# One packed array for the streamed weight tiles, a new start order, and eight unread products

## The chip, the cores and the metric

The kernel runs on one core of a Trainium2 chip. The metric is the device time of one execution in microseconds (us); lower is better. Beside the median of several timed runs there is one profiled execution, from which all rows in this document come.

## The reference

Three blocks run one after the other on x, 256 tokens of width 1024. Only the first steps of the first block matter here; the rest is named.

```python
def ssd_shortconv_layer_mixer(x, w_in, conv_w, conv_b, dt_bias, a_log, d_skip, norm_w, sc_conv_w, w_out):
    proj = x @ w_in
...
    z, xbc, dt_raw = proj[..., :o1], proj[..., o1:o2], proj[..., o2:o3]
    sc_b, sc_c, sc_h = proj[..., o3:o4], proj[..., o4:o5], proj[..., o5:]
    y_ssd = ssd_mixer(z, xbc, dt_raw, conv_w, conv_b, dt_bias, a_log, d_skip, norm_w)
    y_sc = sc_b * causal_dwconv(sc_c * sc_h, sc_conv_w)
    return jnp.concatenate([y_ssd.astype(x.dtype), y_sc.astype(x.dtype)], axis=-1) @ w_out
```

After it come a layer norm, a gated feed-forward layer and a gate (block one, first layer), the same with sliding-window attention (second layer), then a block with two mixers and 32 experts of which each token takes four, then a block with two kinds of attention. `dt_raw` is a product with 16 columns: one per head.

## The kernel before

Everything is float32. x is held transposed, as 128 partitions by 8 groups of features by 256 tokens (`xf`). A product with a weight matrix is made of three products of rounded halves: ScalarE rounds a tile to `wh` (line 295), VectorE or GpSimd subtracts to get `wl` (line 296), x is split in the same way into `xh` and `xl` (`resplit`, lines 707 to 712, by `split`), and TensorE multiplies `xh` by `wh`, `xl` by `wh` and `xh` by `wl` (line 493, reached by `dense_F` and its like).

The weights outside the experts are streamed by the class `Stream`. `weight_plan` lists the tiles in the order in which they are used, as (name, first row, row groups, first column, columns, split or not), and `pieces` cuts them into at most 2048 values per partition, that is, 1 MB. The first tile of the plan has 16 columns and 8 row groups (64 KB): it makes `dt_raw`, in 24 narrow products. Then come two tiles of 512 KB and full tiles. `Stream.load` fills a ring of eight buffers: while there is room, it takes the next tile of the plan and issues its transfer on SyncE's queue. Room is made when the last split of a tile has been issued. The expert tiles are streamed by another class, `Experts`, from arrays that are already contiguous per partition.

The program's order is the order in which the Python code calls the engines; no scheduler reorders it. A transfer whose completion is counted on one of eight semaphores is issued only when the earlier transfer on that semaphore has landed. `run` (from line 2450) issues at the start two transfers of x, of 512 KB each, then `st.load()`; ScalarE issues four small transfers from `consts` (cols, rows, exp_b, positions). `consts` also builds the identity `ident` on VectorE (line 405). Then `ssd_layer` splits x in four quarters and begins with the narrow tile (`dense_F` with n=16, line 752).

In the transfer of a tile, each partition gets one run of n values per row group, n being the tile's columns: 2 KB for 512 columns, 64 bytes for the narrow tile.

Of the kernel before, what the change touches and what calls it, by code (L numbers as in the profile page):

```python
# [22 lines left out]
F32 = mybir.dt.float32  # L23
# [10 lines left out]
T = 256  # L34
# [30 lines left out]
def _cols(v):  # L65
    v = np.asarray(v)
    return np.ascontiguousarray(v.reshape(-1, v.shape[-1] // 128, 128).transpose(2, 0, 1).reshape(128, -1))


def _freq():  # L70

    f = np.ones((128, 2), np.float32)
    for i, half in enumerate((32, 16)):
        inv = (10000.0 ** (-np.arange(half) / half)).astype(np.float32)
        f[:, i] = np.tile(inv, 128 // half)
    return f


def pack(I):
    I = {k: np.asarray(v) for k, v in I.items()}  # L80
    A = {}
    A["xT"] = np.ascontiguousarray(I["x"][0].T)
    A["pT"] = np.ascontiguousarray(I["p"][:, 0].transpose(0, 2, 1))
    hq = np.concatenate([np.arange(h * 64, h * 64 + 64) for h in HPERM])
    A["w_in_mix"] = I["w_in_mix"][0]
    A["w_out_mix"] = I["w_out_mix"][0]
    A["w_qkv"] = np.concatenate([I["w_qkv"][0][:, hq], I["w_qkv"][0][:, 1024:]], axis=1)
    A["w_o"] = np.ascontiguousarray(I["w_o"][0][hq])
    for i in range(2):
        for n in ("w_ffn_gate", "w_ffn_up", "w_ffn_down", "w_ple", "w_ple_gate"):  # L90
            A[f"{n}{i}"] = I[n][i]
    A["ada_p"] = I["ada_w_2"][0][:, :2048]
    A["ada_t"] = np.concatenate([I["ada_w_2"][0][:, 2048:], I["w_ada_3"][0]], axis=1).T
    A["c_rows"] = np.concatenate([I["c_2"], I["c_3"]], axis=1)
    A["w_in_2"] = I["w_in_2"][0]
    A["lora"] = np.concatenate([np.concatenate([I["decay_up_2"][0], I["iclr_up_2"][0]], axis=0), I["gate_up_2"][0]], axis=1)
    A["w_out_2"] = np.concatenate([I["w_out_2"][0][512:], I["w_out_2"][0][:512]])
    A["router_w"] = I["router_w_2"][0]

    A["exp_w1"] = I["exp_w1_2"][0].reshape(32, 4, 2, 128, 2048).transpose(0, 1, 3, 2, 4).reshape(-1, 4096)  # L100
    A["exp_w2"] = I["exp_w2_2"][0].reshape(32, 2, 4, 128, 1024).transpose(0, 1, 3, 2, 4).reshape(-1, 4096)
    A["exp_b1"] = np.ascontiguousarray(I["exp_b1_2"][0].reshape(32, 4, 512).transpose(1, 0, 2)).reshape(128, 512)
    A["exp_b2"] = I["exp_b2_2"][0]
    A["positions"] = I["positions_3"]
    A["w_in_3"] = I["w_in_3"][0]
    A["w_uq"] = I["w_uq_3"][0]
    A["w_ukv"] = I["w_ukv_3"][0]
    A["w_o_mla"] = I["w_o_mla_3"][0]
    A["w_o_moba"] = I["w_o_moba_3"][0]
    A["w_out_3"] = I["w_out_3"][0]  # L110
    bq = I["b_qkv"][0]
    c = {
        "conv_w": _cols(I["ssd_conv_w"][0]), "conv_b": _cols(I["ssd_conv_b"]), "sc_w": _cols(I["sc_conv_w"][0]),
        "ssd_nw": _cols(I["ssd_norm_w"]), "lnm_g": _cols(I["ln_mix_g"]), "lnm_b": _cols(I["ln_mix_b"]),
        "lnf_g": _cols(I["ln_ffn_g"]), "lnf_b": _cols(I["ln_ffn_b"]), "b_ple": _cols(I["b_ple_gate"]),
        "b_qk": _cols(np.concatenate([bq[hq], bq[1024:1280]])), "b_o": _cols(I["b_o"]),
        "d_skip": _cols(np.repeat(I["ssd_d"], 64, axis=1)),
        "norm1_g": _cols(I["norm1_g_2"]), "norm2_g": _cols(I["norm2_g_2"]), "ada_b": _cols(I["ada_b_2"]),
        "mu": _cols(I["shift_mu_2"]), "w0": _cols(I["decay_w0_2"]), "a0": _cols(I["iclr_a0_2"]),
        "k_k": _cols(I["k_k_2"]), "k_a": _cols(I["k_a_2"]), "r_k": _cols(I["r_k_2"].reshape(1, -1)),  # L120
        "lnx_w": _cols(I["lnx_w_2"]), "lnx_b": _cols(I["lnx_b_2"]),
        "q_g": _cols(np.concatenate([I["q_norm_g_2"]] * 2, axis=1)), "k_g": _cols(np.concatenate([I["k_norm_g_2"]] * 2, axis=1)),
        "sb_g": _cols(I["sb_out_g_2"]), "b_ada": _cols(I["b_ada_3"]), "c2": _cols(I["c_2"]), "c3": _cols(I["c_3"]),
        "g_pre": _cols(I["g_pre_3"]), "g_post": _cols(I["g_post_3"]), "g_ql": _cols(I["g_q_lat_3"]),
        "g_kv": _cols(I["g_kv_lat_3"]), "b_merge": _cols(I["b_merge_3"]), "freq": _freq(),
    }
    A["cols"] = np.concatenate([c[k] for k, _ in _COLS], axis=1)
    r = {
        "dt_bias": I["ssd_dt_bias"], "a_log": I["ssd_a_log"],
        "sinks": I["attn_sinks"][:, HPERM], "b_v": I["b_qkv"][:, 1280:],  # L130
        "router_b": I["router_b_2"],
    }
    A["rows"] = np.concatenate([r[k].reshape(1, -1) for k, _ in _ROWS], axis=1)
    return {k: np.ascontiguousarray(v) for k, v in A.items()}


# [91 lines left out]
    return [c for e in P for c in ([e] if e == "end" else pieces(*e))]  # L228


def pieces(name, r0, nk, c0, n, split):

    h = min(nk, 2048 // n)
    return [(name, r0 + k * 128, min(h, nk - k), c0, n, split) for k in range(0, nk, h)]


class Stream:


    def __init__(self, kb, plan, ring=8):  # L240
        self.kb, self.ring = kb, ring
        self.plan = []
        self.units = []
        self.fence = []
        unit = 1024
        for e in plan:
            if e == "end":
                self.fence.append(len(self.units))
                continue
            i = len(self.plan)  # L250
            self.plan.append(e)
            name, r0, nk, c0, n, split = e
            h = nk if not split else max(1, unit // n)
            for k in range(0, nk, h):
                self.units.append((i, k, min(h, nk - k), k + h >= nk, split))
        self.raws = {}
        self.splits = {}
        self.nsplit = self.used = 0
        self.pending = None
        self.rest = kb.nc.vector  # L260
        self.room, self.nload = ring, 0
# [7 lines left out]
            self._retire(self.pending)  # L269
            self.pending = None  # L270

    def load(self):

        kb = self.kb
        while self.room and self.nload < len(self.plan):
            i = self.nload
            self.nload += 1
            self.room -= 1
            name, r0, nk, c0, n, split = self.plan[i]
            t = kb.wpool.tile([128, nk, n], F32, name=f"w_{name}_{i}", tag="w")  # L280
            src = kb.A[name][r0:r0 + nk * 128, c0:c0 + n].rearrange("(k p) n -> p k n", p=128)
            kb.nc.sync.dma_start(t, src)
            self.raws[i] = t

    def _split(self, u):
# [83 lines left out]
class KB:  # L369
    def __init__(self, tc, A, out, stages, dbg=None):  # L370
        self.tc, self.nc, self.A, self.out, self.stages = tc, tc.nc, A, out, stages
        self._dbg = dbg
        self.bg = None
        self.late = (None, None, ())
        self.queue, self.done = [], set()
# [339 lines left out]
    def ssd_layer(self, xf):  # L715
        nc, pp = self.nc, self.pp
        es = ExitStack()
        P = es.enter_context(self.pool("ssd", 1))
        X = self.xpool
        x = self.resplit(xf, X)  # L720

        def padded(n):
# [109 lines left out]
    def state_space(self, P, xs, bc, v):  # L832

        nc, pp, X = self.nc, self.pp, self.xpool
        dt, da, ea, dte = (v[n] for n in ("dt", "da", "ea", "dte"))
# [16 lines left out]
        xdt = self.tl(P, [128, 2, 1024], F32, "xdt")  # L852
        xe = self.tl(X, [128, 2, 1024], F32, "xn")
        xde = xe[:, 0]
# [72 lines left out]
        while not self.x_done:  # L927
            yield
        self.yx = yx = (self.tl(X, [128, 8, T], F32R, "xh"), self.tl(X, [128, 8, T], F32R, "xl"))
        sq = self.tl(X, [128, 8, T], F32, "xn")  # L930
        for k in range(0, 8, 2):
# [83 lines left out]
    def attention(self, P, heads, bias, scale):  # L1015
# [7 lines left out]
        for i in range(n + 3):  # L1023
            if i < n:
# [5 lines left out]
                for b in range(2):  # L1030
                    nc.vector.tensor_reduce(m[:, b:b + 1], p[:, B[b]], axis=AX.X, op=OP.max)  # L1031
                nm = self.tl(P, [128, 2], F32, "an", bufs=2)
# [1417 lines left out]
    def run(self):  # L2450
        nc, tc = self.nc, self.tc
        with ExitStack() as es:
# [17 lines left out]
            self.tl = tl  # L2470
            self.st = Stream(self, weight_plan([n for n in self.stages if n != "third"]))
            xf = self.tl(self.fpool, [128, 8, T], F32, "xf")
            for k in (0, 4):
                nc.sync.dma_start(xf[:, k:k + 4], self.A["xT"][k * 128:k * 128 + 512].rearrange("(k p) n -> p k n", p=128))
            self.st.load()
            nc.scalar.preload_act_table_set("natural_log_exp_and_others")
            self.consts()
# [6 lines left out]
            if "ssd" in self.stages:  # L2484
                xf, x, ready = self.ssd_layer(xf)
                xf, x = self.ffn_ple(0, xf, x, ready)
                self.dbg("xc0", xf)
            else:
                stat = None
                x = self.resplit(xf, self.xpool)  # L2490
            if "att" in self.stages:
                xf, x, ready = self.att_layer(xf, x)
                xf, stat = self.ffn_ple(1, xf, x, ready)
# [7 lines left out]
            if "mix" in self.stages:  # L2501
                xf, stat = self.mixer(xf, stat)
                self.dbg("xd", xf)
            es.close()
            if "moe" in self.stages:
                xf, stat = self.moe(xf, stat)
# [16 lines left out]
ALL = ("ssd", "att", "mod", "mix", "moe", "third")  # L2523
# [14 lines left out]
```

## Time and profile before

| what | before |
|---|---|
| median of 3 runs | 2304.8 us (2302.57 to 2306.72) |
| the profiled execution's own time | 2310.93 us |
| its span, first to last instruction | 2308.8 us |
| TensorE busy | 2149.8 us, 93% |
| VectorE, ScalarE, GpSimd busy | 45%, 31%, 20% |
| mean granted TensorE clock | 0.969 |
| read from memory | 614.9 MB |

The profiled execution is one run of the program, a little slower than the median of the timed runs. Its span leaves out what lies before the first and after the last instruction, 2.1 us here. The busy shares are means over stages with different limits: a share of 93% doesn't say what any one stretch waits for. Expert tiles make up two thirds of the bytes, and they are read in the span's second half.

### The profile page before, as it was taken

To read this page: it belongs to the slowest core of one execution; us is meant where nothing else is said; L and a number is where in the kernel's file an instruction comes from. 1 tells how busy PE (TensorE), PEld (TensorE's weight loads), DVE (VectorE), ACT (ScalarE), POOL (GpSimd) and SP (SyncE) were. 2 spreads that over 40 slices of the span, in tenths; PEclk is the share of its full clock that TensorE was granted. 3 is DMA by queue.
4 is the path that set the end of the run, shared out by engine and by line. 5 is a ranking of instruction groups with operands and counts; after the bars stand their busy time and mean duration, and the time that the engine had idled before them with its cause. 6 is when DMAs were issued, how large, how long until landed. Compare 5 with 4: busy or idle time off the path is not lost.

```text
span 2308.8 us, 31649 instructions
## 1 busy us (share of the span) xinstructions
PE 2149.8 (93%) x13226; PEld 1513.6 (66%) x13226; DVE 1034.6 (45%) x1937; ACT 725.8 (31%) x1169; POOL 454.1 (20%) x220
## 2 busy tenths in 40 slices
PE   7999999989999987888899999999999999989996
PEld 7897898887898887778444444344433333367886
DVE  6674676555677658755222222322222211133653
ACT  5434544445544553333111111111111111033542
POOL 2322232233232234221000000000000000046454
PEclk9999999999999989989999999999999999999998
DMA  8434777532777632204799999999999999964320
GB/s 294 158 128 142 265 252 282 186 128 68 264 257 285 242 122 89 74 1 173 320 427 427 427 423 427 428 427 427 427 428 427 427 428 427 427 225 143 113 71 19
DMA packets 122339, 618.05 MB, mean 268 GB/s; under 512 B 8624, under 2 KB 17712, under 8 KB 97616
## 3 DMA queue, kind: packets, MB, share of 16 engines
q1 hardware_dynamic: 119008, 612.33, 67.6%
q10 hardware_dynamic: 3184, 3.65, 0.5%
q8 instruction: 106, 1.74, 0.3%
q14 instruction: 41, 0.34, 0.0%
HBM read 614.90 MB, written 1.05 MB: 267 GB/s over the span
## 4 chain that ended last, share of the span: by engine, by line
PE 34%; DMA 12%; DVE 3%; issue 1%; ACT 1%; POOL 0%; ACTq 0%; DVEq 0%; POOLq 0%; SPq 0%
PE acc L493 21%; DMA expert<-exp_w 12%; PE py L493 10%; PE tp L493 2%; DVE an L1034 1%; PE tp L2015 0%; POOL wl L296 0%; DVE pr L1065 0%; ACT pr L1057 0%; DVE am L1031 0%; PE tp L2007 0%; DVE qf L2443 0%; DVE ot L2377 0%; DVE r4h L505 0%; DVE kz L2350 0%
## 5 line engine op out<-in xcount | busy, mean ns | idle before, releaser
L493 PE MATMUL acc<-xh,wh 128*128 128x256 f32 (+1 forms) x1736 | 498.8, 291 | 16.1 <-ACT wh L295 13.3
L493 PE MATMUL acc<-xh,wl 128*128 128x256 f32 (+2 forms) x1704 | 488.5, 287 | 21.1 <-POOL wl L296 11.7
L493 PE MATMUL acc<-xl,wh 128*128 128x256 f32 (+1 forms) x1736 | 491.9, 287 | 0.6 <-DVE xl L1263 0.5
L493 PE MATMUL acc<-expert,xe 128*64 128x512 f32 x2048 | 457.4, 597 | 19.2 <-DMA expert<-exp_w 17.1
L493 PEld LDWEIGHTS acc<-xh,wh 128*128 128x128 f32 (+1 forms) x1736 | 332.2, 193 | 25.0 <-ACT wh L295 13.9
L493 PEld LDWEIGHTS acc<-xh,wl 128*128 128x128 f32 (+2 forms) x1704 | 328.2, 193 | 26.0 <-POOL wl L296 14.1
L493 PEld LDWEIGHTS acc<-expert,xe 128*64 128x64 f32 x2048 | 144.6, 137 | 301.2 <-issue 282.2
L493 PEld LDWEIGHTS acc<-xl,wh 128*128 128x128 f32 (+1 forms) x1736 | 333.2, 193 | 4.2 <-issue 1.4
L296 POOL TENSOR_TENSOR wl<-w_w_in,wh 128x1024 fp32r<-128x1024 f32 (+1 forms) x49 | 119.2, 2442 | 1080.6 <-DMA w_w_in<-w_in 950.1
L493 PE MATMUL py<-expert,aT 128*64 128x512 f32 x1024 | 235.3, 602 | 6.3 <-DMA expert<-exp_w 5.5
L1990 ACT ACTIVATE s<-a 128x512 f32<-128x512 f32 x32 | 20.1, 630 | 531.3 <-DVE a L1989 531.3
L2050 DVE SCALAR_TENSOR_TENSOR xf<-py,mod,xf 128x256 f32<-128x256 f32 x128 | 55.6, 479 | 282.4 <-PE py L493 282.4
L1989 DVE TENSOR_SCALAR a<-acc 128x512 f32<-128x512 f32 x32 | 22.1, 691 | 347.6 <-PE acc L493 347.6
L493 PEld LDWEIGHTS py<-expert,aT 128*64 128x64 f32 x1024 | 71.9, 138 | 140.8 <-issue 128.7
L1206 DVE SCALAR_TENSOR_TENSOR w_ada_t<-w_ada_t,pe 128x1024 f32<-128x1024 f32 x56 | 93.2, 1687 | 0.0
L295 ACT ACTIVATE wh<-w_w_in 128x1024 fp32r<-128x1024 f32 (+1 forms) x66 | 68.5, 1046 | 39.4 <-PE acc L493 35.9
L2037 ACT ACTIVATE y<-py 64x512 f32<-64x512 f32 x64 | 37.9, 592 | 121.0 <-PE py L493 120.4
L493 PE MATMUL tp<-sel,xh 128*128 128x128 f32 x512 | 63.5, 285 | 7.9 <-ACT aT L2017 6.9
L493 PE MATMUL acc<-wh,hh 128*128 128x512 f32 x176 | 68.7, 390 | 0.0
L295 ACT ACTIVATE wh<-w_w_ffn_down 128x1024 fp32r<-128x1024 f32 x44 | 46.8, 1064 | 69.3 <-PE acc L493 69.3
L493 PE MATMUL acc<-wh,hl 128*128 128x512 f32 x176 | 68.5, 389 | 0.0
L493 PE MATMUL acc<-wl,hh 128*128 128x512 f32 x176 | 68.5, 389 | 0.0
(657 smaller groups left out, 3406.4 us busy)
## 6 DMA issues: line engine op xcount, KB each, us to landing
expert<-exp_w SPq DMA_DIRECT2D x192, 2048.0 KB, 30.4
w_w_in<-w_in SPq DMA_DIRECT2D x31, 1024.0 KB, 5.1
w_ada_t<-ada_t SPq DMA_DIRECT2D x28, 1024.0 KB, 7.0
w_w_ffn_gate<-w_ffn_gate SPq DMA_DIRECT2D x22, 1024.0 KB, 5.2
w_w_ffn_up<-w_ffn_up SPq DMA_DIRECT2D x22, 1024.0 KB, 6.0
w_w_ffn_down<-w_ffn_down SPq DMA_DIRECT2D x22, 1024.0 KB, 5.7
w_w_in_mix<-w_in_mix SPq DMA_DIRECT2D x21, 1024.0 KB, 8.7
w_w_out_mix<-w_out_mix SPq DMA_DIRECT2D x8, 1024.0 KB, 4.9
```

The source lines that it names most:

```text
L295: kb.nc.scalar.activation(hi, w, AF.Copy)
L296: (kb.nc.gpsimd if u % 3 == 0 else self.rest).tensor_sub(lo, w, hi.bitcast(F32))
L493: self.nc.tensor.matmul(out, lhsT, rhs, start=start, stop=True, skip_group_check=True)
L1034: nc.vector.tensor_scalar(nm, m, -scale, None, op0=OP.mult)
L1206: self.nc.vector.scalar_tensor_tensor(w[:, j], w[:, j], 1.0, crow[:, int(m >= 48)], op0=OP.mult, op1=OP.mult, accum_out=dst)
L1989: nc.vector.tensor_scalar(a, pg, 7.0, None, op0=OP.min)
L1990: nc.scalar.activation(s, a, AF.Sigmoid, scale=1.702)
L2037: nc.scalar.activation(y[r, o], py[r], AF.Copy)
L2050: nc.vector.scalar_tensor_tensor(xf[:, k], ps[o][:, c], gate2(k), xf[:, k], op0=OP.mult, op1=OP.add)
```

## The change

Four things are done in it.

- The streamed tiles are packed into one array, `tiles`, one tile after the other, each with its values in the order of partition, row group, column. A tile is then one contiguous run per partition: 8 KB for a full tile, 4 KB for those of 512 KB, 512 bytes for the narrow one. `places` gives the offset of each tile.
- x is packed as 128 x 8 x 256, and is read in four transfers of two groups each, in runs of 2 KB (before: two transfers of four groups, in runs of 1 KB).
- `load` gets a limit `n` on the number of tiles; `run` calls `load(1)` ahead of x and `load()` behind it.
- `ssd_layer` begins with eight products of the identity with itself into a PSUM tile that nobody reads.

```diff
@@ pack
-    A["xT"] = np.ascontiguousarray(I["x"][0].T)
+    A["xT"] = I["x"][0].T.reshape(8, 128, T).transpose(1, 0, 2)
...
+    flat = [A[e[0]][e[1]:e[1] + e[2] * 128, e[3]:e[3] + e[4]].reshape(e[2], 128, e[4]).transpose(1, 0, 2).reshape(-1) for e in places()]
+    for name in {e[0] for e in places()}:
+        del A[name]
+    A["tiles"] = np.concatenate(flat)
...
+def places():
+
+    at, n = {}, 0
+    for e in weight_plan(ALL):
+        if e != "end" and e not in at:
+            at[e] = n
+            n += 128 * e[2] * e[4]
+    return at
@@ Stream
-    def load(self):
+    def load(self, n=999):
 
         kb = self.kb
-        while self.room and self.nload < len(self.plan):
+        while self.room and self.nload < min(n, len(self.plan)):
             i = self.nload
             self.nload += 1
             self.room -= 1
-            name, r0, nk, c0, n, split = self.plan[i]
+            name, _, nk, _, n, split = self.plan[i]
             t = kb.wpool.tile([128, nk, n], F32, name=f"w_{name}_{i}", tag="w")
-            src = kb.A[name][r0:r0 + nk * 128, c0:c0 + n].rearrange("(k p) n -> p k n", p=128)
-            kb.nc.sync.dma_start(t, src)
+            o = kb.places[self.plan[i]]
+            kb.nc.sync.dma_start(t.rearrange("p k n -> p (k n)"), kb.A["tiles"][o:o + 128 * nk * n].rearrange("(p m) -> p m", p=128))
             self.raws[i] = t
@@ ssd_layer
+
+        warm = self.tl(pp, [128, 128], F32, "tp")
+        for _ in range(8):
+            self.mm(warm, self.ident, self.ident, start=True)
         x = self.resplit(xf, X)
@@ run
-            for k in (0, 4):
-                nc.sync.dma_start(xf[:, k:k + 4], self.A["xT"][k * 128:k * 128 + 512].rearrange("(k p) n -> p k n", p=128))
+            self.st.load(1)
+            for k in range(0, 8, 2):
+                nc.sync.dma_start(xf[:, k:k + 2], self.A["xT"][:, k:k + 2])
             self.st.load()
```

How this moves instructions is seen at two places. First SyncE's queue at the start of the program. `xf` is x, `w_w_in_mix` with a number is a tile of the stream's ring; the brackets name the semaphore that an issue waits for. Before:

```order
L2474 DMA xf_75<-xT 128x4x256 x2
L282 DMA w_w_in_mix_78<-w_in_mix 128x8x16
L282 DMA w_w_in_mix_80<-w_in_mix 128x2x512
L282 DMA w_w_in_mix_82<-w_in_mix 128x2x512 [waits DMAHW0_49]
L282 DMA w_w_in_mix_84<-w_in_mix 128x4x512 [waits DMAHW1_49]
L282 DMA w_w_in_mix_86<-w_in_mix 128x4x512 [waits DMAHW2_49]
L282 DMA w_w_in_mix_88<-w_in_mix 128x4x512 [waits DMAHW3_49]
L282 DMA w_w_in_mix_90<-w_in_mix 128x4x512 [waits DMAHW4_49]
L282 DMA w_w_in_mix_92<-w_in_mix 128x4x512 [waits DMAHW5_49]
L282 DMA w_w_in_mix_144<-w_in_mix 128x4x512 [waits DMAHW6_49,Pool_49]
```

And the changed kernel:

```order
L296 DMA w_w_in_mix_76<-tiles 128x128
L296 DMA w_w_in_mix_78<-tiles 128x1024
L296 DMA w_w_in_mix_80<-tiles 128x1024
L296 DMA w_w_in_mix_82<-tiles 128x2048
L296 DMA w_w_in_mix_84<-tiles 128x2048 [waits DMAHW0_49]
L296 DMA w_w_in_mix_86<-tiles 128x2048 [waits DMAHW1_49]
L296 DMA w_w_in_mix_88<-tiles 128x2048 [waits DMAHW2_49]
L296 DMA w_w_in_mix_90<-tiles 128x2048 [waits DMAHW3_49]
L2494 DMA xf_75<-xT 128x512 [waits DMAHW4_49]
L2494 DMA xf_75<-xT 128x512 [waits DMAHW5_49]
L2494 DMA xf_75<-xT 128x512 [waits DMAHW6_49]
L2494 DMA xf_75<-xT 128x512 [waits DMAHW7_49]
```

x stood ahead of all eight tiles of the ring before; now all eight stand ahead of x.

The second place is ScalarE's first work, the splits of x and of the first tiles (the four issues of constants stand ahead of it in both). Before:

```order
L531 ACTIVATE xh_127<-xf_75 128x512 [waits DMAHW0_49]
L531 ACTIVATE xh_127<-xf_75 128x512
L531 ACTIVATE xh_127<-xf_75 128x512 [waits DMAHW2_49]
L531 ACTIVATE xh_127<-xf_75 128x512
L295 ACTIVATE wh_140<-w_w_in_mix_78 128x128 [waits DMAHW5_49]
```

And the changed kernel:

```order
L546 ACTIVATE xh_138<-xf_75 128x512 [waits DMAHW4_49]
L546 ACTIVATE xh_138<-xf_75 128x512 [waits DMAHW5_49]
L546 ACTIVATE xh_138<-xf_75 128x512 [waits DMAHW6_49]
L546 ACTIVATE xh_138<-xf_75 128x512 [waits DMAHW7_49]
L309 ACTIVATE wh_151<-w_w_in_mix_76 128x128 [waits DMAHW0_49]
```

The sequence is the same; each quarter of x now has a transfer of its own to wait for, and the narrow tile's split still stands behind all four.

## Rows read from the trace of the kernel before

**Rows 1.** The page: the span, and each engine's busy time.

```profile
span 2308.8 us, 31649 instructions
...
PE 2149.8 (93%) x13226; PEld 1513.6 (66%) x13226; DVE 1034.6 (45%) x1937; ACT 725.8 (31%) x1169; POOL 454.1 (20%) x220
```

**Rows 2.** Who waited for whom: us in total, times, longest; whole span.

```profile
POOL wl L296 <- DMA w_w_in<-w_in: 950.1, 1, 950.1
...
PE acc L493 <- ACT wh L295: 15.6, 5, 11.2
PE acc L493 <- POOL wl L296: 15.5, 11, 1.9
PE acc L493 <- DVE wl L296: 11.0, 11, 2.7
...
ACT xh L531 <- DMA xf<-xT: 5.6, 2, 3.1
...
ACT wh L295 <- DMA w_w_in_mix<-w_in_mix: 2.2, 3, 1.0
```

**Rows 3.** Timeline from 0 to 12 us: start, duration, instruction, idle before.

```profile
1.13 0.23 DVE L405 TENSOR_SCALAR ident<-xn 128x128 f32<-128x128 int32 x1 [1.13 <-POOL xn L403]
...
5.17 1.15 ACT L531 ACTIVATE xh<-xf 128x512 fp32r<-128x512 f32 x2 [3.14 <-DMA xf<-xT]
...
8.80 1.15 ACT L531 ACTIVATE xh<-xf 128x512 fp32r<-128x512 f32 x2 [2.48 <-DMA xf<-xT]
...
10.81 0.31 ACT L295 ACTIVATE wh<-w_w_in_mix 128x128 fp32r<-128x128 f32 x1 [0.86 <-DMA w_w_in_mix<-w_in_mix]
...
11.17 0.40 PE L493 MATMUL acc<-xh,wh 128*16 128x256 f32 x1 [11.17 <-ACT wh L295]
```

**Rows 4.** Busy time by engine, granted clock, DMA, in stretches of the start.

```profile
11.00:16.20 5.20, 5.03 (x24) 3.17 (x25) 2.45 (x2) 2.24 (x3) 0.46 (x1) 1.00 1.05 395
16.20:30.00 13.80, 13.41 (x112) 13.04 (x111) 4.95 (x14) 7.20 (x15) 4.79 (x3) 1.00 1.04 386
```

**Rows 5.** DMA view: 10 to 40 us, then 1300 to 1400 us.

```profile
DMA packets 5945, 11.64 MB, mean 388 GB/s; under 512 B 272, under 2 KB 273, under 8 KB 5944
...
DMA packets 2956, 42.45 MB, mean 425 GB/s; under 512 B 341, under 2 KB 341, under 8 KB 373
```

**Rows 6.** DMA view, single issues: those at 0.75, 1.25, 1.80, 11.02, 15.63 us.

```profile
xf<-xT SPq DMA_DIRECT2D x1, 512.0 KB, 4.4
...
xf<-xT SPq DMA_DIRECT2D x1, 512.0 KB, 7.5
...
w_w_in_mix<-w_in_mix SPq DMA_DIRECT2D x1, 64.0 KB, 9.0
...
w_w_in_mix<-w_in_mix SPq DMA_DIRECT2D x1, 1024.0 KB, 16.0
...
w_w_in_mix<-w_in_mix SPq DMA_DIRECT2D x1, 1024.0 KB, 15.3
```

**Rows 7.** DMA view, 0 to 12 us: rate in 40 slices, issues of constants.

```profile
GB/s 0 0 0 0 0 0 72 181 123 212 274 331 379 376 382 369 384 328 238 264 303 377 359 348 244 175 121 124 199 256 236 271 317 360 399 430 382 410 410 410
...
b<-exp_b ACTq DMA_DIRECT2D x1, 256.0 KB, 7.3
cols<-cols ACTq DMA_DIRECT2D x1, 193.5 KB, 3.6
rows<-rows ACTq DMA_DIRECT2D x1, 168.0 KB, 5.9
rope<-positions ACTq DMA_DIRECT2D x1, 128.0 KB, 8.2
```

**Rows 8.** The page's costly groups: count, busy, mean ns, idle before.

```profile
L493 PE MATMUL tp<-sel,xh 128*128 128x128 f32 x512 | 63.5, 285 | 7.9 <-ACT aT L2017 6.9
```

**Rows 9.** Stretches of the third part's start, columns as in rows 4.

```profile
2040.50:2045.30 4.80, 0.66 (x2) 0.29 (x2) 3.87 (x18) 0.50 (x2) 1.22 (x1) 0.50 0.85 325
2045.30:2049.40 4.10, 4.04 (x17) 3.81 (x18) 4.03 (x10) 3.00 (x7) 0.00 (x0) 0.50 0.01 5
```

More of the change, by code (lines that the diff above doesn't have):

```diff
@@ L372, in __init__ @@
         self._dbg = dbg
+        self.places = places()
         self.bg = None
```

## The prediction

> **What bounds the kernel now.** I read the page first. TensorE is busy for 93% of the span [rows 1]. The chain that ended last is traced only from the second half on, so it says nothing about the part that this change edits. What remains is the list of waits. In it I look for two things: waits of any engine for a weight tile or for x, and waits of TensorE in the first 230 us. For a streamed tile or x there are only three entries: ScalarE waited 5.6 us for x in two waits and 2.2 us for tiles of `w_in_mix` in three, and GpSimd's 950 us in one wait is the expert part, in which it has no tile to split [rows 2]. So outside the first microseconds no engine waits for a streamed tile: the ring of eight buffers hides them. At the start TensorE waits 11.2 us in one wait, for ScalarE's split `wh` [rows 2].
>
> The timeline of the start shows why. The two halves of x are issued first (0.75 and 1.25 us), then the narrow tile (1.80 us) and the rest [rows 6]. ScalarE splits x at 5.17 and 8.80 us, when its halves have landed, then the narrow tile at 10.81 us, and the first product starts at 11.17 us [rows 3]. The 24 narrow products fill the time to 16.2 us (5.03 us busy of 5.20), and from there TensorE is the limit: 13.41 us busy of 13.80 [rows 4]. What delays the first product therefore delays everything behind it, and whatever lands earlier than now after 16 us is worth nothing.
>
> **The layout of the tiles.** No copy is added on the chip, and each tile has the same size as before. Only the contiguous run grows, from n values to 8 KB for a full tile. In the start, where the queue is never empty, 11.64 MB went in 5945 packets at 388 GB/s; in the expert part, whose tiles are contiguous already, 42.45 MB in 2956 packets at 425 GB/s [rows 5]. That saves 0.23 us on each 1 MB tile (1.0486 MB at 388 is 2.70 us, at 425 it is 2.47). I cost it at nothing from 16 us on: the ring hides it. If that cover were gone, the price in the open is bounded by the 2.2 us of tile waits [rows 2], which all lie in the start.
>
> **The order on SyncE's queue.** The words of the change say that the narrow tile goes first, then x. The program's order says something else: all eight tiles of the first ring stand ahead of the four transfers of x. The reason is one line: `load(self, n=999)` unpacks `name, _, nk, _, n, split` inside its loop, so after the first tile n is that tile's 16 columns and no longer the limit 1, and the loop goes on until the ring is full. `load(1)` is thus a full load, and the `load()` after x finds no room.
>
> Does that matter, or do transfers of one queue run side by side? They land in the order of issue, one at a time. The issues at 0.75, 1.25 and 1.80 us landed 4.4, 7.5 and 9.0 us later, at 5.15, 8.75 and 10.8 us; the eighth tile, issued at 11.02 us, landed 16.0 us later, at 27.0 us [rows 6]. The next one, issued at 15.63 us, took 15.3 us, to 30.9 us [rows 6]. So x will land about when the eighth tile lands now, since the same bytes are ahead of it: 64 KB, two of 512 KB, five of 1024 KB, x of 1024 KB, and 745.5 KB from ScalarE's queue (cols, rows, exp_b, positions), together 7977.5 KB or 8.17 MB [rows 7].
>
> The landing of the last quarter of x, step by step from 27.0 us:
> - The narrow tile now costs 10.8 - 8.75 = 2.05 us for 64 KB. With 512 B runs I give it 64 KB at 388 GB/s, 0.17 us: 1.9 us saved, 25.1 us.
> - Seven tiles, 6.29 MB, at 425 in place of 388 GB/s: 16.2 - 14.8 = 1.4 us saved, 23.7 us.
> - x in runs of 2 KB in place of 1 KB. Only the start itself bears on it (x and most of ScalarE's bytes took from 1.8 to 8.75 us). I take 0.5 us saved, an estimate: **23.2 us**.
>
> The bounds: all 8.17 MB at 425 GB/s from the first bytes at about 1.8 us [rows 7] gives 21.0 us; only the narrow tile's saving gives 25.1. The nearer row is the present landing of the same bytes, so I stay by it.
>
> The Trainium skill's page DMA: Bandwidth & Descriptors, in "Anatomy of one DMA — SWDGE (gpsimd) path", fits a transfer as 2.0 us plus its bytes at 436 GB/s, for transfers of another issuing path than these. By that x would land at 0.75 + 2.0 + 18.7 = 21.5 us, and the sum below would be 11.3 us and not 13.0; the rows of the start, 388 GB/s, do not bear it out, and no row of this kernel tests its fixed part.
>
> The issues of x also wait, each for an earlier transfer that has the same semaphore (the row order names the semaphore). Those are tiles and constants among the first eight transfers; the last of them is the fourth tile, some 2.9 MB into the queue or about 9 us. The queue then still holds 4 to 5 MB, so these waits cost nothing. Behind x nothing waits on SyncE but the ninth tile, which needs a buffer that is freed only by a split.
>
> **From x to the first product.** ScalarE's order is four splits of x, then the narrow tile. Behind the last quarter: one `xh` of some 0.6 us (a pair takes 1.15), then 0.36 us from the narrow `wh` to the first product (10.81 to 11.17) [rows 3], about 1.0 us with the wait's release. TensorE starts at 23.2 + 1.0 = 24.2 us in place of 11.2: **+13.0 us**. Four splits in place of two pairs are no more work: there are four now as well. VectorE's last `xl` and the first wide `wl` are ready within 2.6 us, while the narrow products take 5.0. The tiles are all in SBUF by then, so no stall follows, but there is no idle to win back either: from 16.2 to 30 us TensorE idled 0.4 us [rows 4].
>
> **The eight unread products.** The nearest row is 128x128 products of the same type, 63.5 us for 512, 0.124 us each, 0.25 at half the clock [rows 8]: 2 us in all. They need only the identity, which VectorE writes at 1.13 us [rows 3], so they run from about 1.5 to 3.5 us beside the transfers and cost nothing. Their gain hangs on the clock. The narrow products run for 5.03 us, 24 of them at 0.21 us; the next 112 at 0.12 us [rows 4]. The record says 1.00 for that stretch, but so wide a spacing is found where it says 0.50, the 1.2 GHz level: 17 products in 4.04 us, 0.24 us each [rows 9]. Full clock for the 24 would save 5.0 - 24 x 0.12 = 2.1 us. But in the third part the granted clock is 0.50 in a stretch in which TensorE had 0.66 us of work in 4.8 us, and it is still 0.50 in the next, although TensorE is busy there for 4.04 us of 4.10 [rows 9]. Here 20 us without a product lie between the unread ones and the first real one. I take no gain.
>
> **The sum.** Layout 0, order +13.0, products 0. On the profiled execution's own time, 2310.9 us, that makes 2323.9; that execution lies 6.1 us over the median of the runs, 2304.8 us, and all its terms carry over: **2317.8 us**, slower by 0.56%.
>
> **Rivals.**
> 1. *The clock stays up*: the 2.1 us are saved, 2315.7 us. Against it: the clock fell where TensorE had little to do [rows 9]. Chance 0.06.
> 2. *Tiles are late all along*, so faster landing pays. TensorE waits for splits: 15.6 us (of which 11.2 at the start), 11.0 and 15.5 us, so 30.9 us beyond the start [rows 2]. If all of it hung on landings that now come in time, the total would be 2304.8 + 13.0 - 30.9 = 2286.9 us. It decides from 13 us of these 30.9 on. Against it: the splits themselves waited only 2.2 us for tiles. Chance 0.03.
> 3. *The change does as it says*: narrow tile and x ahead. Then x lands with 64 KB more and fewer short packets ahead, at 7.5 to 8.7 us; the first product starts at 8.5 to 9.7 us, 1.5 to 2.7 us earlier, and with the clock up 2.1 more: 2300 to 2303.3 us. Against it stands the order. Chance 0.03.
> 4. *x slips past the tiles* because the queue serves several transfers side by side. The last x is issued at about 9 us and can land at 11 to 14 us: TensorE 1 to 4 us later, 2306 to 2309 us. Against it: the landings in order [rows 6]. Chance 0.04.
>
> **How the numbers follow.** My forecast has 0.84. Its bounds are 21.0 and 25.1 us for x, so +10.8 to +14.9 us; with 1 us of scatter of the median (the three runs span 4.1 us) that is 2314 to 2321. The range 2312 to 2321 takes in the first rival too. A measurement of this kernel tells about 0.2%, 4.6 us, from no change. Faster by more: rival 2 and a third of rival 3, 0.04. Within: the rest of 3 and rival 4, 0.06. Slower: 0.90.
>
> **What would show it.** In the changed profile: eight tile issues, then four of x on SyncE; the four `xh` between about 20 and 24 us; the eight `tp` products alone at 1.5 to 3.5 us; the first real product near 24 us with the narrow ones still 0.21 us apart; from 60 us on the same stretches of work, shifted. A first product before 12 us, or a second part that is shorter, would make it wrong.

## The result and the profile after

The changed kernel takes 2316.7 us (median of 5 runs, 2316.56 to 2318.72), the kernel before 2306.5 us (median of 5). The ratio, which is not the quotient of the two medians, is 1.0052, with a 95% interval of 1.0038 to 1.0066. The change makes the kernel slower by 10.2 us in the medians and by 12.0 us by the ratio (8.8 to 15.2 us in the interval). The forecast was 2317.8 us, slower by 13.0.

The page of the changed kernel shows a longer span than [rows 1], at a slightly smaller busy time of TensorE, so what was added to the span is waiting:

```profile
span 2314.5 us, 31684 instructions
...
PE 2142.5 (93%) x13242; PEld 1507.0 (65%) x13242; DVE 1035.6 (45%) x1937; ACT 724.6 (31%) x1169; POOL 452.5 (20%) x220
```

The list of waits says where: ScalarE's wait for x grew from 5.6 to 20.2 us, and TensorE's longest wait for `wh` from 11.2 to 20.1 us, answering to [rows 2]. TensorE's wait is counted here from the end of the unread products, at 5.0 us, so its first real product is later by more than these two waits differ.

```profile
PE acc L508 <- ACT wh L309: 23.3, 4, 20.1
...
ACT xh L546 <- DMA xf<-xT: 20.2, 1, 20.2
```

The timeline of the start, answering to [rows 3] (start, duration, instruction, idle before):

```profile
0.75 7.30 SPq L296 DMA_DIRECT2D w_w_in_mix<-tiles  x8
...
1.41 3.59 PE L508 MATMUL tp<-ident 128*128 128x128 f32 x16 [1.41 <-DVE ident L420]
...
8.57 5.70 SPq L2494 DMA_DIRECT2D xf<-xT  x4
22.26 2.60 ACT L546 ACTIVATE xh<-xf 128x512 fp32r<-128x512 f32 x4 [20.23 <-DMA xf<-xT]
...
24.77 2.19 ACT L309 ACTIVATE wh<-w_w_in_mix 128x128 fp32r<-128x128 f32 x3
25.11 0.39 PE L508 MATMUL acc<-xh,wh 128*16 128x256 f32 x1 [20.11 <-ACT wh L309]
...
29.71 0.28 PE L508 MATMUL acc<-xh,wh 128*128 128x256 f32 x1
```

Eight tiles are issued, then the four quarters of x from 8.57 us on. x is split from 22.26 us, the first real product starts at 25.11 us in place of 11.17, and the first wide one (128 weight columns in place of 16) at 29.71 us, 13.4 us later than the 16.27 us of before.

The DMA view of the changed kernel, for 2 to 6, 6 to 20 and 20 to 25 us, and the last transfer of x alone (issued at 13.84 us; the last number is the time to landing):

```profile
DMA packets 506, 0.93 MB, mean 231 GB/s; under 512 B 47, under 2 KB 376, under 8 KB 506
...
DMA packets 1134, 5.92 MB, mean 423 GB/s; under 512 B 129, under 2 KB 271, under 8 KB 525
...
DMA packets 623, 1.30 MB, mean 261 GB/s; under 512 B 80, under 2 KB 80, under 8 KB 592
...
xf<-xT SPq DMA_DIRECT2D x1, 256.0 KB, 10.4
```

From 6 us on the full tiles flow at 423 GB/s, faster than the 388 of [rows 5]. From 2 to 6 us the rate is only 231 GB/s, and x lands last, at 13.84 + 10.4 = 24.2 us.

The clock, in the windows view (stretch; its length; busy time and count of TensorE, weight loads, VectorE, ScalarE and GpSimd; granted clock; DMA share; GB/s):

```profile
4.70:8.10 3.40, 0.30 (x3) 0.11 (x1) 0.00 (x0) 0.00 (x0) 0.00 (x0) 1.00 0.99 315
8.10:25.10 17.00, 0.00 (x0) 0.00 (x0) 2.18 (x4) 2.75 (x6) 0.00 (x0) 0.50 0.92 373
25.10:28.50 3.40, 3.15 (x15) 1.83 (x15) 2.85 (x3) 1.86 (x2) 0.76 (x1) 0.50 0.42 125
28.70:45.00 16.30, 15.81 (x132) 15.30 (x131) 4.95 (x14) 8.69 (x17) 4.83 (x3) 1.00 0.66 235
```

The clock is full just after the unread products, at half (1.2 GHz) while TensorE waits, and still at half for the first fifteen of the narrow products.

### The profile page after: what moved, and what is told of

It is laid out like the page before. It is cut to its first block, busy times and chain, and to the rows that moved or that the text cites. A ratio compares the mean times of both kernels' runs of the same rounds, so it can differ in the third digit from the quotient of the medians.

```text
span 2314.5 us, 31684 instructions
## 1 busy us (share of the span) xinstructions
PE 2142.5 (93%) x13242; PEld 1507.0 (65%) x13242; DVE 1035.6 (45%) x1937; ACT 724.6 (31%) x1169; POOL 452.5 (20%) x220
## 4 chain that ended last, share of the span: by engine, by line
PE 32%; DMA 13%; DVE 3%; issue 1%; ACT 1%; POOL 0%; ACTq 0%; DVEq 0%; SPq 0%; POOLq 0%
PE acc L508 20%; DMA expert<-exp_w 13%; PE py L508 9%; PE tp L508 2%; DVE an L1053 1%; PE tp L2034 0%; POOL wl L310 0%; DVE pr L1084 0%; ACT pr L1076 0%; DVE am L1050 0%; PE tp L2026 0%; DVE qf L2462 0%; DVE ot L2396 0%; DVE r4h L520 0%; DVE kz L2369 0%
## 5 line engine op out<-in xcount | busy, mean ns | idle before, releaser
L508 PEld LDWEIGHTS acc<-xh,wl 128*128 128x128 f32 (+2 forms) x1704 | 326.4, 192 | 25.1 <-POOL wl L310 14.2
L2009 ACT ACTIVATE s<-a 128x512 f32<-128x512 f32 x32 | 20.2, 630 | 530.5 <-DVE a L2008 530.5
```

Source lines behind the costliest of these rows:

```text
L508: self.nc.tensor.matmul(out, lhsT, rhs, start=start, stop=True, skip_group_check=True)
L2009: nc.scalar.activation(s, a, AF.Sigmoid, scale=1.702)
```

## The experiments

The theory: x's place in the queue is the whole slowdown; the layout and the products add nothing to it. The rivals: the packed layout itself costs time, or the products do, or the layout pays later on. All runs are compared with runs of the kernel before on the same chip.

**The order alone, in the kernel before** (old layout, no products):

```diff
+            self.st.load()
             for k in (0, 4):
                 nc.sync.dma_start(xf[:, k:k + 4], self.A["xT"][k * 128:k * 128 + 512].rearrange("(k p) n -> p k n", p=128))
-            self.st.load()
```

> The kernel before with one edit: the ring of eight tiles is filled ahead of x; layout as before, no unread products. Theory (the place of x in the queue is the whole slowdown): the same bytes as before end at about 27 us, so x lands at 26 to 27 us, the first narrow product starts near 28 us, 16 to 17 us later than before, and the time is 2318 to 2324 us, more than the changed kernel's 2316.7. Rival (the packed layout costs the time): near 2306.5 us.

Measured: 2321.5 us, ratio 1.0068 (1.0055 to 1.0081). Its timeline:

```profile
12.56 5.59 SPq L2475 DMA_DIRECT2D xf<-xT  x2
...
27.13 1.15 ACT L531 ACTIVATE xh<-xf 128x512 fp32r<-128x512 f32 x2 [0.23 <-DMA xf<-xT]
...
28.53 0.40 PE L493 MATMUL acc<-xh,wh 128*16 128x256 f32 x1 [28.53 <-ACT wh L295]
```

x lands at 27.1 us, as the eighth tile did before [rows 6], and the first product starts at 28.53 us. The order by itself makes the kernel slow, by 15 us in the medians. Against it the changed kernel's first product is 3.4 us earlier.

These two kernels have the same order of transfers and another layout, so together they size the layout's share. The DMA view, first for the narrow tile in the run with the order alone and in the changed kernel (time from issue to landing), then for 6 to 20 us with the order alone:

```profile
w_w_in_mix<-w_in_mix SPq DMA_DIRECT2D x1, 64.0 KB, 3.3
...
w_w_in_mix<-tiles SPq DMA_DIRECT2D x1, 64.0 KB, 2.6
...
DMA packets 2743, 5.22 MB, mean 373 GB/s; under 512 B 125, under 2 KB 262, under 8 KB 2743
```

At the head of the queue the narrow tile lands 0.7 us sooner with the longer runs, the full tiles flow at 423 in place of 373 GB/s, and x lands 2.9 us sooner (24.2 against 27.1 us).

**The changed kernel without the unread products** (the three lines of `warm` left out):

> The changed kernel without the eight unread products. Theory (they end 20 us ahead of the first real product and do nothing): first narrow product at 25 us and 0.21 us apart as with them, time within 2 us of 2316.7. Rival (the products keep the clock or cost time): more than 3 us away on either side.

Measured: 2319.8 us, ratio 1.0061 (1.0048 to 1.0074), whose interval overlaps the changed kernel's. In the timeline the first and the last narrow product, 24 in all:

```profile
25.30 0.40 PE L508 MATMUL acc<-xh,wh 128*16 128x256 f32 x1 [25.30 <-ACT wh L309]
...
30.60 0.41 PE L508 MATMUL acc<-xh,wl 128*16 128x256 f32 x1
```

They start where they did with the products. All 24 run at the wide spacing here, where nine of them were at the narrow one in the changed kernel; the first wide product comes at 30.81 in place of 29.71 us. That 1.1 us is not shown to be the products' work: the run with the layout alone, next, has no products either, and eight of its 24 narrow products run at the narrow spacing, so the moment of the rise varies without them. The medians lie 3.1 us apart, over the 2 us that were expected at most and just over the 3 us that the rival asked for, but the two intervals overlap. What the products do to the time stays open to within these 3 us.

**The layout alone** (x and its two transfers as before, ahead of all tiles; no products):

```diff
...
-            self.st.load(1)
-            for k in range(0, 8, 2):
-                nc.sync.dma_start(xf[:, k:k + 2], self.A["xT"][:, k:k + 2])
+            for k in (0, 4):
+                nc.sync.dma_start(xf[:, k:k + 4], self.A["xT"][k * 128:k * 128 + 512].rearrange("(k p) n -> p k n", p=128))
             self.st.load()
```

> Only the packed tiles; x in its two transfers of before and ahead of all tiles, no unread products. Theory: the narrow tile lands right behind x, at about 9 us in place of 10.8, the first narrow product starts near 9.5 us, 1.5 to 2 us earlier, and nothing else moves: 2304 to 2305.5 us. Rival (the layout costs): above 2310 us. Rival (tiles are late all along, so the layout pays later): below 2300 us.

Measured: 2304.9 us, ratio 1.0001 (0.9987 to 1.0014): no change. The time is as expected, the reason is not:

```profile
9.89 1.15 ACT L546 ACTIVATE xh<-xf 128x512 fp32r<-128x512 f32 x2 [3.53 <-DMA xf<-xT]
...
11.65 0.31 ACT L309 ACTIVATE wh<-w_w_in_mix 128x128 fp32r<-128x128 f32 x1 [0.62 <-DMA w_w_in_mix<-tiles]
...
12.02 0.40 PE L508 MATMUL acc<-xh,wh 128*16 128x256 f32 x1 [12.02 <-ACT wh L309]
```

The narrow tile did not land earlier. It still came 1.8 us behind x, as 512-byte runs, and the first product started at 12.02 us, 0.85 us later than before. So the 2 us behind x were not the price of the 64-byte runs. The layout neither costs 10 us nor pays anything later, which the last run below shows more sharply.

**The order as the words say** (the limit in a variable of its own):

```diff
-    def load(self, n=999):
+    def load(self, most=999):
...
-        while self.room and self.nload < min(n, len(self.plan)):
+        while self.room and self.nload < min(most, len(self.plan)):
```

> The changed kernel with the limit of load kept in a variable of its own, so that the narrow tile goes first, then the four transfers of x, then the other tiles. Theory: x lands by 7.5 to 8.7 us, the first narrow product starts at 8.5 to 9.7 us, 1.5 to 2.7 us earlier than before: 2303.5 to 2305 us, and 2.1 us less if the clock is up. Rival (something else in the change costs 10 us): near 2314 us.

Measured: 2304.1 us, ratio 0.9987 (0.9975 to 1.0000). In the timeline and the windows view:

```profile
9.73 0.63 ACT L546 ACTIVATE xh<-xf 128x512 fp32r<-128x512 f32 x1 [0.22 <-DMA xf<-xT]
...
10.61 0.39 PE L508 MATMUL acc<-xh,wh 128*16 128x256 f32 x1 [5.41 <-ACT wh L309]
```

```profile
5.60:8.70 3.10, 0.00 (x0) 0.00 (x0) 0.69 (x1) 1.06 (x2) 0.00 (x0) 1.00 1.02 369
8.70:10.60 1.90, 0.00 (x0) 0.00 (x0) 1.56 (x3) 1.61 (x4) 0.00 (x0) 0.50 0.92 371
10.60:15.50 4.90, 4.66 (x22) 2.85 (x23) 2.93 (x3) 2.12 (x2) 0.76 (x1) 0.50 1.03 431
```

One variable's name takes the whole loss away, which settles the cause, and the time is as expected. But x lands at 9.7 us and not at 7.5 to 8.7, so the first product gains 0.6 us and not 1.5 to 2.7, and the first wide one, at 15.85 us, gains 0.4. The clock is full behind the eight products, until 8.7 us. It fell 1.9 us before the first real product.

**Ninety unread products in the changed kernel** (`range(90)`):

> The changed kernel with 90 unread products in place of 8, enough to keep TensorE busy from 1.4 us to about 24 us. Theory (8 products fail because 20 us without work follow them): the clock is up when the first real product starts at 25 us, the 24 narrow products are 0.12 us apart, the first wide product starts 2 us earlier than in the changed kernel, at 27.5 to 28 us in place of 29.7, and the time is 1.5 to 2.5 us below 2316.7. Rival (unread products do nothing for the clock): narrow products 0.21 us apart again, no gain.

Measured: 2321.0 us, ratio 1.0060 (1.0037 to 1.0082): no gain, and 4.3 us above the changed kernel in the medians. In its windows view:

```profile
4.80:23.40 18.60, 18.50 (x166) 18.31 (x164) 0.00 (x0) 0.00 (x0) 0.00 (x0) 1.00 0.99 396
23.40:26.60 3.20, 0.00 (x0) 0.00 (x0) 2.10 (x4) 2.74 (x6) 0.00 (x0) 1.00 0.07 27
26.60:28.50 1.90, 1.46 (x11) 0.97 (x12) 1.44 (x2) 1.86 (x2) 0.76 (x1) 1.00 0.22 26
28.70:32.00 3.30, 3.30 (x17) 2.58 (x16) 1.20 (x2) 0.50 (x2) 0.00 (x0) 0.51 0.94 335
```

The clock was full when the real products began, as the theory says, but the products had ended 3.3 us earlier. After eleven narrow products, 1.46 us of work, it fell to half in the midst of work and stayed there until 31.9 us, and the gain was gone. That the idle time ahead of them brought the fall is a reading; no run shows it by itself. Besides, x was split from 23.84 us here, 1.6 us later than in the changed kernel, and the first real product came at 26.61 us in place of 25.11 and the first wide one at 31.26 in place of 29.71; why x was late in this profile stays open.

**Twenty-four products with the order as said** (both edits together):

> The order that the words of the change say, with 24 unread products in place of 8, which end at about 9 to 11 us, near the first real product at 10.6 us. Theory: narrow products 0.12 us apart, first wide product at 13.4 to 14 us in place of 15.9, and 2 us below the same kernel with 8 products: near 2302 us. Rival: the products outlast the landing of x (at half clock they take 10.8 us in all, to 12.2 us) and the gain is given back: 2304 us or more.

Measured: 2305.7 us, ratio 0.9998 (0.9984 to 1.0012). In its windows view:

```profile
10.20:13.60 3.40, 2.93 (x24) 2.10 (x24) 0.52 (x2) 1.06 (x1) 0.75 (x1) 1.00 1.01 420
...
19.00:23.50 4.50, 2.86 (x24) 2.68 (x24) 3.79 (x12) 1.76 (x7) 0.87 (x1) 1.00 1.01 419
...
24.00:27.20 3.20, 3.20 (x17) 3.20 (x16) 1.23 (x1) 0.46 (x1) 0.00 (x0) 0.50 1.00 415
```

The unread products end at 9.59 us, 0.65 us ahead of the first real one. The narrow products now run at full clock, 24 in 2.93 us, and the wide ones begin at 13.66 us, as expected and 2.2 us earlier than with 8 products. The lead is lost within the next microseconds: VectorE's step `dw` at line 829, on which a later product depends, starts at 19.94 us here and at 19.91 with 8 products, in both just behind GpSimd's split `wl`, which runs from about 17.5 to 19.9 us in both (that the one holds the other is not shown). TensorE had work for only 2.86 of 4.50 us, waiting 1.6 us of it for VectorE, and then the clock fell at 24 us for 3.2 us of full work. Neither the expected 2 us nor any other gain is left in the time. The time is the one that the rival named, but not by its mechanism: the products did not outlast the landing of x.

**The constants out of x's way.** To the run above, two edits in `consts`:

```diff
-        nc.scalar.dma_start(self.b1, self.A["exp_b1"])
+        nc.sync.dma_start(self.b1, self.A["exp_b1"])
...
-        nc.scalar.dma_start(self.posi, bass.AP(tensor=a.tensor, offset=a.offset, ap=[[0, 128], [1, T]]))
+        nc.sync.dma_start(self.posi, bass.AP(tensor=a.tensor, offset=a.offset, ap=[[0, 128], [1, T]]))
```

> The kernel of the run above with two more edits: the transfers of exp_b and positions (384 KB, needed only in later parts) go to SyncE's queue behind the eight tiles. Theory (x lands late because ScalarE's transfers share the engines with it): 0.39 MB at 388 GB/s is 1.0 us, x's last quarter lands at 8.7 us in place of 9.7, and the first real product starts at 9.6 us, or when the unread products end if that is later; 1 us less than the run above, near 2301 us. Rival (the two transfers do not hold x): no change.

Measured: 2304.3 us, ratio 0.9986 (0.9971 to 1.0000). In the timeline, and in the windows view:

```profile
8.36 0.63 ACT L546 ACTIVATE xh<-xf 128x512 fp32r<-128x512 f32 x1 [0.18 <-DMA xf<-xT]
...
9.24 0.29 PE L508 MATMUL acc<-xh,wh 128*16 128x256 f32 x1
```

```profile
9.20:12.60 3.40, 2.97 (x25) 2.16 (x25) 2.28 (x3) 2.13 (x2) 0.76 (x1) 1.00 1.03 434
12.60:30.00 17.40, 16.51 (x138) 16.18 (x137) 7.34 (x17) 10.17 (x18) 4.82 (x3) 1.00 1.01 416
```

x's last split moved from 9.36 us in the run above to 8.36 us, by the 1.0 us expected, and the clock held. The first product starts 1.9 us earlier than before and the wide ones 3.6 us. The time is not the 2301 us that were expected: of the 3.6 us the medians show 1.3 and the ratio 3.2, with an interval from nothing to 6.7.

**The kernel before, once more.**

> The kernel before, unchanged, profiled a second time. Theory (where the clock falls to half between 40 and 1110 us differs from execution to execution, and that is what moved the difference of the two first profiles from 13.4 us after the start to 5.5 us at the end): the half-clock stretches in that part add up to another sum than in the first profile, 55 to 80 us against 82, and the second half of the program starts some us earlier or later than in the first profile, with the same start. Rival (the packed layout gave 8 us back later): the same times as in the first profile to within 1 us.

Measured: 2305.7 us, ratio 1.0001 (0.9983 to 1.0019). In the chain that ended last, one and the same piece of the expert part starts at 1135.45 us in the first profile of before:

```profile
1135.45 16.46 PE acc L493 x68
```

and in the second:

```profile
1125.16 16.46 PE acc L493 x68
```

Two executions of one program, whose first wide products are 0.05 us apart (16.27 and 16.22 us), are 10.3 us apart there. The first difference between them shows where this comes from. In the first profile, one instruction of VectorE, a stretch of the windows view behind it, and a later instruction of VectorE:

```profile
119.79 0.69 DVE L922 TENSOR_TENSOR xs<-xs,z 128x512 f32<-128x512 f32 x1
...
125.30:128.80 3.50, 3.48 (x19) 3.15 (x20) 3.46 (x7) 0.00 (x0) 0.86 (x1) 0.51 0.71 287
...
132.08 1.07 DVE L898 TENSOR_TENSOR M<-M,cbm 128x512 f32<-128x512 f32 x1 [2.48 <-ACT M L897]
```

The same of the second:

```profile
119.77 0.69 DVE L922 TENSOR_TENSOR xs<-xs,z 128x512 f32<-128x512 f32 x1
...
123.80:127.20 3.40, 1.91 (x19) 1.74 (x20) 3.40 (x5) 1.12 (x2) 2.33 (x2) 1.00 0.67 204
...
130.54 1.07 DVE L898 TENSOR_TENSOR M<-M,cbm 128x512 f32<-128x512 f32 x1 [0.96 <-ACT M L897]
```

Nineteen products take 3.48 us at half clock in the one and 1.91 us at full clock in the other, and behind them the two executions are 1.5 us apart where they were 0.02 apart. Every later step of more than 0.4 us, up to the expert part, lies likewise at a stretch that is at half clock in one of the two and not, or for a shorter time, in the other. From 40 to 1110 us the stretches with a granted clock of 0.50 add up to 87.0 us in the first profile (the expectation has 82) and to 54.6 in the second, just under the 55 to 80 that were expected.

So each profile can be taken apart into its start, up to the first wide product, and the stretch from there to the first product of the expert part, with the part of it that is at half clock (all in us):

| profile | first wide product | expert part starts | between | of it at half clock |
|---|---|---|---|---|
| before, first | 16.27 | 1115.88 | 1099.6 | 88.8 |
| before, second | 16.22 | 1105.59 | 1089.4 | 54.6 |
| order as said, 8 products | 15.85 | 1105.21 | 1089.4 | 54.6 |
| layout alone | 16.44 | 1107.80 | 1091.4 | 64.9 |
| changed kernel | 29.71 | 1121.15 | 1091.4 | 64.9 |
| order alone | 33.90 | 1126.48 | 1092.6 | 61.5 |
| without the products | 30.81 | 1124.45 | 1093.6 | 78.5 |
| constants late, 24 products | 12.65 | 1108.79 | 1096.1 | 75.1 |
| 90 products | 31.26 | 1128.39 | 1097.1 | 86.0 |
| order as said, 24 products | 13.66 | 1113.69 | 1100.0 | 78.5 |

In two pairs of these the stretches at half clock lie at the same work and are equally long: before, second, and order as said with 8 products; the layout alone and the changed kernel. There the stretch between is the same to 0.1 us, with the tiles packed as without, and with x last as with x first. So the layout pays nothing behind the start, and a shift of the start is carried in full to the expert part. The sum alone doesn't fix the time: 78.5 us stands beside 1093.6 and beside 1100.0, at other work, and in the latter the lead was lost at a wait besides. The 8 us that seemed to come back between the start and the end of the changed kernel's profile (13.4 us late after the start, 5.7 us in the span) were not given back by the change: the first profile of before, at 2310.93 us against a median of 2305.6, has more half-clock time than any other here. And the run with the late constants kept its lead over the second profile of before, 3.1 us, until 176 us, and had lost it by 199 us, behind two stretches at half clock that the other profile doesn't have.

## Why the prediction was right

*The order.* The step that carried the forecast held: the program issues eight tiles ahead of x, transfers of one queue land in turn, and TensorE waits for the end of it. The run with the order alone, and the one with the variable renamed, show it from both sides.

*The landing of x.* Forecast 23.2 us, bounds 21.0 and 25.1; measured 24.2: the layout moved the landing by 2.9 us (27.1 to 24.2) where 3.8 were forecast. Of its three terms, the faster tiles are confirmed (423 GB/s against the 425 assumed). The narrow tile's 1.9 us was mis-sized: the longer runs saved 0.7 us at the head of the queue and nothing behind x. The 0.5 us for x's own longer runs was tried by no run alone. What the 2 us behind x are instead stays open; moving 384 KB of ScalarE's constants away moved x by 1.0 us, so transfers of that queue take time from x, but that they held the narrow tile is not shown. The 21.5 us estimated from the fit in the Trainium skill's page DMA: Bandwidth & Descriptors ("Anatomy of one DMA — SWDGE (gpsimd) path") are not borne out: x landed 2.7 us later, and from 2 to 6 us the rate was 231 GB/s.

*From x to the first product.* Forecast 1.0 us, measured 25.11 - 24.2 = 0.9 us. The start shifted by 13.9 us, against 13.0.

*The products.* No gain was taken, and none is shown. They took 3.6 us in place of the 2 forecast, since each is two entries in the trace, and the 512 of [rows 8] are entries too, of 256 products. Beside the transfers that cost nothing. The rival in which the clock stays up fell: the clock was at half from 8.1 us on. The narrow products took 4.6 us in place of 5.1, since the clock rose earlier among them, which the layout alone shows as well. That they ran at half clock before was rightly read from their spacing: the clock's record of the first profile begins at 16.1 us, and the 1.00 of [rows 4] for the stretch ahead of it says nothing.

*The layout.* Costed at nothing from 16 us on, and the run with it alone gives 1.0001. The rival in which tiles are late all along falls with it, and with the equal stretches of the table at the end of the experiments.

*The other rivals.* The change does not do as it says; made to, it takes 2304.1 us, just above the 2300 to 2303.3 that this rival gave, since x lands 1 us later than assumed. And x did not slip past the tiles: it landed last of all.

*The sum.* 13.0 us forecast; 10.2 in the medians, 12.0 by the ratio, with 13.0 inside the interval. The table gives it more sharply: 13.3 us from the layout alone to the changed kernel, whose half-clock stretches are the same, and 0.2 us from the second profile of before to the layout alone, together 13.5. That the sum comes so near is in part luck: x landed 1.0 us later than forecast, and the narrow products took 0.5 us less. What the forecast had too small is the scatter: it allowed 1 us for the median, and the profiles of one program differ by 10 us at the same place.

## What to carry to other kernels

Read the order of the built program before costing a change to it: a loop variable that shadows a parameter turned "x first" into "x last", and no line of the change's description tells it. In a queue that serves transfers in turn, what the first work needs belongs at the front; of the 17.4 us that the order alone added to the first product, layout and products gave back 3.4. Unread products that ended 0.65 us ahead of the real work had the clock up for it, those that ended 3.3 us ahead lost it 1.9 us into the work, and even where it held, a lead at the start can be lost at the next wait. One profile is no base for a difference of a few us: compare executions piece by piece, and first see whether the clock was the same.

## What the runs showed of the hardware

Raising the clock at the start did not carry: with 90 products it was full at the first real product and fell 1.9 us later, in the midst of work (granted 0.51), after 3.3 us without any; with 24 it fell at 24 us, after a stretch with 2.86 us of work in 4.50. Where it falls differs between executions of one program, and with it the start of the expert part, by 10.3 us in two profiles of before: the two part only at stretches that are at half clock in one of them and not as long in the other, 87.0 us against 54.6 in all. Why it falls there in one execution and not in the other stays open.

The Trainium skill's page TensorE: Matmul & The Clock Gate, in "Part 1: The HAM clock gate", says of the warm-up at a kernel's start that it varies from run to run and is worth under 1% of a typical span. The traces agree at the start: in the five profiles without unread products 16 to 24 of the 24 narrow products ran at the wide spacing, and the first wide one started 4.4 to 5.5 us behind the first narrow one. What moved the time more, the 10.3 us, or 0.4% of the span, came along the way, of which that passage doesn't speak.
